# Weights made ready one product ahead, and a norm stage without GpSimd, in a one-core two-layer block

## The chip, the cores and the metric

The kernel runs on one core of one Trainium2 chip. The number that counts is the device time of one execution in microseconds. A core has five engines that run side by side and wait for one another by semaphores: TensorE (PE, matmuls, with a separate track PEld for loading its stationary operand), VectorE (DVE), ScalarE (ACT), GpSimd (POOL) and SyncE (SP), whose queue issues most DMAs.

## The reference, cut to what matters

One block on a sequence of 1024 tokens of width 1024, all in float32. First comes a gated DeltaNet with 8 heads of 128 and an MLP, then a final norm of the stream, then a second layer (a norm with modulation, a mixer that also reads projections of a 256-row context, a second MLP). What the change touches:

```
# DeltaNet
proj = h @ w_in                                   # q, k, v, z: 1024 columns each
q, k, v = silu(causal_depthwise_conv(proj[:3072]))# 4 taps
lower = strict(k_beta k^T * decay); solve (I + lower) [u, w] = [...]   # per 64-token chunk
state scan over 16 chunks; o = rms(o) * norm_w * silu(z)
x = x + o @ w_out                                 # part of w_out: dn_w_out[0:768]
# MLP of the first layer
x = x + square(relu(rms(x) @ w_up)) @ mlp_w_down
# between the layers: x1 = rms(x) * norm_final, then the modulated norm of x1 for layer 2
x1 = x * r1 * wf ;  h2 = x * a * r12 + sh
ctx projections: 14 products of the normed context (256 rows) with columns of w_in_2
```

Here r1 and r12 are reciprocal roots of column sums of squares (of x, and of x times wf), spread over the 128 partitions as rows.

## The kernel before, in words

Everything lies transposed: a tile is 128 features (partitions) by 512 or 1024 tokens. Matmuls keep float32 accuracy by splitting every operand into a rounded high part and a low rest: `gemm` (L149 to L151) issues three matmuls per 128 rows of weights, high by high, high by the low part of the data, and low by high. So a product with 1024 rows of weights over 512 tokens is 24 matmuls of 128x512, always in the order L149, L150, L151.

The weights of a product come from `wload`, three steps on three engines: a DMA of the raw weights on SP's queue (L138), a cast of them to the high part on ACT (L139, tile `whi`), and a subtraction on DVE that leaves the low part (L140, tile `wlo`). L149 and L150 need `whi` alone, L151 needs `wlo`. There are two buffers each for raw, high and low. A new product's raw weights can be fetched when the subtraction of the product two before has read its raw buffer.

The order of the instructions on each engine is settled when the program is built: a scheduler places them one by one, led by the order of the source, its own estimate of when operands are there, and when buffers come free. What an engine then runs is one fixed row; an instruction that waits holds up all behind it on that engine.

The stages that the change touches, in order of time in the span:

- **DeltaNet, 40 to 600 us.** Heads are worked in four pairs. For a pair: `keys` (two k projections, `project` L272, with the copy of a product out of PSUM at L285, the four-tap convolution as L288 and L290 on DVE, and silu on ACT, L292), `norms_k` (transposes L326, squares L329, the roots of L336), `prep_k` in `base` (the decay matrix `dec` L363 to L370, the products of keys L376, the matrix `N` L377, and the DMAs of its small blocks to memory and back as `A`, L382), `invert_base` (a chain of some 60 small DVE steps L396 and L400 on the 32x32 blocks `X`, which go to memory (Xd) and back as X, L415), `values` (v and q projections), `place_base` (L426 to L452, small matmuls that build the inverse `TT`, with gate products as filler between them), and `scan` (L509 to L529). While a pair is scanned, the next pair's keys and bases are made, and its v and q projections run on PE beside the DVE chain L396/L400.
- **The output projection, 600 to 690 us** (L673 to L684): 8 products with 768 rows of `dn_w_out`, each two halves of 18 matmuls. The results are copied out of PSUM by DVE (first half) and ACT (second half), L680. Beside it DVE works off the modulation vectors: long runs of L898 and L900 (`macc`), with L907 and L909 at the end of a run.
- **The first layer's last down group, 1345 to 1420 us** (`down_group`, L836, called with `done`): 16 products, 12 matmuls each, of 128 columns, the first token half first. After each, DVE adds it to x (L849), ACT squares x twice (L709), and the two sums of squares go on: one on POOL (tile `e`, L710), one on DVE (tile `fs`, L710).
- **The norms between the layers, 1410 to 1480 us** (`FirstNorms.half`, run once for each token half): sums to columns (L717, L718), roots on ACT (L202), rows (L726, L728), and then for each of 8 feature tiles f: e = x a r12 on DVE (L984), high part on ACT (L985), x r1 on POOL (L986), times wf on ACT (L987), a DMA of it out (L988), and the low part on DVE (L978). Between these steps run the 14 context products (`ctx_project` L1032), 24 matmuls of 128x256, whose weights are loaded when the product is written down; result copied by ACT, L1039. Five of them have buffers of their own for the weights (`wx`).

Of the kernel before, what the change touches and what calls it, by code (L numbers as in the profile page):

```python
# [11 lines left out]
AF = mybir.ActivationFunctionType  # L12
ALU = mybir.AluOpType
# [15 lines left out]
WX = (10, 8, 6, 4, 2)  # L29
# [176 lines left out]
def deltanet(k, spill, dbg=None):  # L206

    nc, tc, A = k.nc, k.tc, k.A
    with ExitStack() as ctx:
# [3 lines left out]
        load = load_normed(k, P, hhi, hlo)  # L213
# [4 lines left out]
        ps = k.pt((128, 96))  # L218
# [6 lines left out]
        w_in = A["dn_w_in"]  # L225
# [6 lines left out]
        W = k.wload(w_in[:, 4096:4112], cols=16)  # L232
        ps = k.pt((128, 8, 16))
        for i, sl in enumerate(HALVES):
# [21 lines left out]
            out=gl, in0=t1, scalar=-1.0, in1=ab[:, 0:1, :].to_broadcast([128, 8, 8]), op0=ALU.mult, op1=ALU.mult)  # L256
        ps = k.pt((128, 8, 8))
# [11 lines left out]

        pair = {}  # L270

        def project(h, part, out):  # L272

            W = k.wload(w_in[:, part * 1024 + h * 128: part * 1024 + h * 128 + 128])
            n = part * 8 + h
            prev = None
            for i, sl in enumerate(HALVES):
                ps = k.pg()
                k.gemm(ps, W, hhi, hlo, sl)
                pre = P.tile([128, 516], F32, tag="pre", name=k.nm("pre"), bufs=2)  # L280
                if prev is None:
                    nc.gpsimd.memset(pre[:, 0:4], 0.0)
                else:
                    nc.scalar.copy(pre[:, 0:4], prev[:, 512:516])
                nc.scalar.copy(pre[:, 4:516], ps)  # L285
                prev = pre
                acc = P.tile([128, 512], F32, tag="acc", name=k.nm("acc"), bufs=2)
                nc.vector.tensor_scalar(acc, pre[:, 4:516], convw[:, 3, n:n + 1], None, op0=ALU.mult)  # L288
                for t in (2, 1, 0):
                    nc.vector.scalar_tensor_tensor(out=acc, in0=pre[:, 1 + t:513 + t], scalar=convw[:, t, n:n + 1],  # L290
                                                   in1=acc, op0=ALU.mult, op1=ALU.add)
                nc.scalar.activation(out(i), acc, AF.Silu)  # L292
                yield
# [255 lines left out]
                    nc.vector.tensor_tensor(out=lo[:, sl], in0=z[:, sl], in1=hi[:, sl], op=ALU.subtract)  # L549

        def gates(h, pr):
            W = k.wload(w_in[:, 3072 + h * 128:3072 + h * 128 + 128])
            pr["z", h] = z = (k.xp if h % 2 else P).tile([128, 1024], F32, tag=("z", "xA")[h % 2], name=k.nm("z"), bufs=1)
            for i, sl in enumerate(HALVES):
                ps = k.pg()
                yield from k.gemm_steps(ps, W, hhi, hlo, sl)
                nc.scalar.activation(z[:, sl], ps, AF.Silu)
# [68 lines left out]
        gated = {}  # L626
# [4 lines left out]
        for p in range(4):  # L631
            pr = pair[p]
            hs = (2 * p, 2 * p + 1)
            solutions(p)
            if p == 3:
                for h in hs:
                    gated[h] = tuple(k.s1.tile([128, 1024], F32R, tag="s1", name=k.nm("o" + c)) for c in "hl")
                for h in range(6):
                    o = k.wp.tile([128, 1024], F32, tag="raw", name=k.nm("o2"), bufs=2)
# [30 lines left out]

        ms = mod.stream([0, 1, 2], [t[:, j] for t in raws for j in range(2)], nc.gpsimd, tmp)
        x = []
        for o in range(8):  # L673
            tag = ("xN", "xN", "xA", "xX", "xe", "xe", "xTT", "xTT")[o]
            x.append(k.xp.tile([128, 1024], F32, tag=tag, name=k.nm("x"), bufs=1 if tag in ("xA", "xX") else 2))
            W = k.wload(A["dn_w_out"][0:768, o * 128:o * 128 + 128], nk=6)
            for i, sl in enumerate(HALVES):
                ps = k.pg()
                k.gemm(ps, W, [gated[h][0] for h in range(6)], [gated[h][1] for h in range(6)], sl)
                (nc.scalar.copy if i else nc.vector.tensor_copy)(x[o][:, sl], ps)  # L680
                next(ms, None)
                next(ms, None)
# [5 lines left out]
HALVES = [slice(0, 512), slice(512, 1024)]  # L688
# [42 lines left out]
def dn_out_and_mlp(k, gated, mod, norms, cpd, x2d, ud, td):  # L731

    nc, A = k.nc, k.A
    x = k.x
    with ExitStack() as ctx:
        s1, s2 = k.s1, k.s2
# [62 lines left out]
        h0, cx = [], []  # L799
# [23 lines left out]
        down_group(k, A["mlp_w_down"][3584:4096], [h for h, _ in hidden], [l for _, l in hidden], xs, done=done,  # L823
                   cols=128)
        tiles = list(CTX_TILES)
        for _ in chain(h0[0], norms.half(1, HALVES[1])):
            if tiles:
                ctx_project(k, *cx, cpd, tiles.pop(0), (s1, "s1") if len(tiles) in WX else None)
        for n in tiles:
            ctx_project(k, *cx, cpd, n)  # L830


def down_group(k, wd, uhi, ulo, x, scale=None, done=None, cols=256, hook=None):


    nc = k.nc  # L836
    n = len(uhi)
    for hs in ([[0], [1]] if done is not None else [[0, 1]]):
        for o2 in range(1024 // cols):
            W = k.wload(wd[:, o2 * cols:o2 * cols + cols], nk=n, cols=cols)  # L840
            for j in range(cols // 128):
                o = cols // 128 * o2 + j
                Wj = (W[0][:, :, 128 * j:128 * j + 128], W[1][:, :, 128 * j:128 * j + 128])
                for i in hs:
                    sl = HALVES[i]
                    ps = k.pg()
                    k.gemm(ps, Wj, uhi, ulo, sl)
                    if scale is None:
                        nc.vector.tensor_tensor(out=x[o][i], in0=x[o][i], in1=ps, op=ALU.add)  # L849
                    else:  # L850
                        nc.vector.scalar_tensor_tensor(out=x[o][i], in0=ps, scalar=scale[:, o:o + 1],
                                                       in1=x[o][i], op0=ALU.mult, op1=ALU.add)
                    if done is not None:
                        done(o, i, sl)
                    if hook:
                        hook()
# [75 lines left out]
class FirstNorms:  # L932
# [15 lines left out]

    def add(self, o, i, sl):
        xs = self.x[o][:, sl]  # L950
        self.s1.add(i, xs)
        self.s2.add(i, xs, scale=self.wf[:, o:o + 1], eng=self.k.nc.vector)

    def half(self, i, sl):
        k, nc, P, x, wf, hhi, hlo = self.k, self.k.nc, self.P, self.x, self.wf, self.hhi, self.hlo
        if i == 0:
            g1 = k.vec["g_norm1_2"]
            self.a, self.sh = affine(k, g1, k.mod[:, 0:8], k.mod[:, 8:16], "a1")
            nc.vector.tensor_tensor(out=self.a, in0=self.a, in1=wf, op=ALU.mult)
        a, sh = self.a, self.sh  # L960
        c1 = P.tile([128, 4], F32, tag="c1", name=k.nm("c1"), bufs=1)
        c2 = P.tile([128, 4], F32, tag="c2", name=k.nm("c2"), bufs=1)
        if i == 0:
            self.r = self.s1p.tile([128, 2, 512], F32, tag="s1", name=k.nm("r"))
        r, nt = self.r, {}
        r1, r12 = r[:, 0, :], r[:, 1, :]
        yield
        self.s1.cols(i, c1)
        self.s2.cols(i, c2)
        rstd_cols(k, c1, c1, D, P)  # L970
        nc.vector.tensor_tensor(out=c2, in0=c2, in1=c1, op=ALU.mult)
        nc.vector.tensor_tensor(out=c2, in0=c2, in1=c1, op=ALU.mult)
        rstd_cols(k, c2, c2, D, P)
        nc.vector.tensor_tensor(out=c2, in0=c2, in1=c1, op=ALU.mult)
        rows(k, c2, r12)
        rows(k, c1, r1)
        def low(f):
            nc.vector.scalar_tensor_tensor(out=hlo[f][:, sl], in0=nt.pop(f), scalar=sh[:, f:f + 1],  # L978
                                           in1=hhi[f][:, sl], op0=ALU.add, op1=ALU.subtract)

        for f in range(8):
            xs = x[f][:, sl]
            t = nt[f] = k.e()
            nc.vector.scalar_tensor_tensor(out=t, in0=xs, scalar=a[:, f:f + 1], in1=r12, op0=ALU.mult, op1=ALU.mult)  # L984
            nc.scalar.activation(hhi[f][:, sl], t, AF.Identity, bias=sh[:, f:f + 1])  # L985
            nc.gpsimd.tensor_tensor(out=xs, in0=xs, in1=r1, op=ALU.mult)  # L986
            nc.scalar.activation(xs, xs, AF.Copy, scale=wf[:, f:f + 1])  # L987
            nc.sync.dma_start(self.x1d[f][:, sl], xs)  # L988
            if f:
                low(f - 1)  # L990
            yield
        low(7)
# [36 lines left out]
        yield  # L1029


def ctx_project(k, chi, clo, cpd, n, pool=None):  # L1032

    nc = k.nc
    W = k.wload(k.A["w_in_2"][:, 128 * n:128 * n + 128], pool=pool)
    ps = k.pg()
    k.gemm(ps[:, 0:256], W, chi, clo, slice(0, 256))
    t = k.e()[:, 0:256]
    nc.scalar.copy(t, ps[:, 0:256])  # L1039
    nc.scalar.dma_start(cpd[n], t)  # L1040
# [836 lines left out]
class Down:  # L1877
# [19 lines left out]
    def load(self, g, m):  # L1897

        k, nc = self.k, self.k.nc
        p0, n = self.groups[g]  # L1900
        for j in range(n):
            t = self.T[Up.OPERAND[m]][j]
            nc.sync.dma_start(t[:, 1].bitcast(F32), self.td[p0 + j][Up.OPERAND[m]])
        self.late.append((g, m))
        if len(self.late) > 3:
            self.split()
# [283 lines left out]
```

## Time and profile before

| what | value |
|---|---|
| median of 3 runs | 2970.7 us (2970.43 to 2975.29) |
| the profiled execution | 2967.41 us, span 2965.4 us |
| PE busy | 2790.5 us, 94% of the span |
| DVE, ACT, POOL busy | 70%, 48%, 22% |
| mean granted clock of PE | 0.983 |

The profile is of one execution, 3.3 us below the median. 2.0 us of it lie outside its span. A wait of PE is read in two ways in the rows below: as a row of the view of waits (engine, line, what it waited for: us in total, times, the longest), and in the timeline, where the bracket behind an instruction gives the idle time before it and what ended it. The mean granted clock of a stretch (PEclk) says how much of it PE spent at the lower of its two levels.

### The profile page before, as it was taken

To read this page: it belongs to the slowest core of one execution; us is meant where nothing else is said; L and a number is where in the kernel's file an instruction comes from. 1 tells how busy PE (TensorE), PEld (TensorE's weight loads), DVE (VectorE), ACT (ScalarE), POOL (GpSimd) and SP (SyncE) were. 2 spreads that over 40 slices of the span, in tenths; PEclk is the share of its full clock that TensorE was granted. 3 is DMA by queue.
4 is the path that set the end of the run, shared out by engine and by line. 5 is a ranking of instruction groups with operands and counts; after the bars stand their busy time and mean duration, and the time that the engine had idled before them with its cause. 6 is when DMAs were issued, how large, how long until landed. Compare 5 with 4: busy or idle time off the path is not lost. (4 is left out here: it accounts for less than half of the span.)

```text
span 2965.4 us, 43793 instructions
## 1 busy us (share of the span) xinstructions
PE 2790.5 (94%) x16344; PEld 2275.9 (77%) x16344; DVE 2088.1 (70%) x3343; ACT 1409.0 (48%) x2690; POOL 644.8 (22%) x578
## 2 busy tenths in 40 slices
PE   7999999989899999999899998999899999999998
PEld 5887878777677777787777777788777788887776
DVE  5877777785888887777856657677757755556784
ACT  6452636433555563435633334677645433334345
POOL 0000000011132333222422222121020322332322
PEclk9999999999899999999999999999999999999999
DMA  4313131234366774442621111001033433234433
GB/s 112 69 32 72 30 71 46 72 115 155 124 208 226 232 251 134 149 146 71 195 62 38 42 51 46 12 29 61 15 122 113 132 97 100 98 122 171 136 115 110
DMA packets 330084, 310.16 MB, mean 105 GB/s; under 512 B 36640, under 2 KB 254720, under 8 KB 329872
## 3 DMA queue, kind: packets, MB, share of 16 engines
q1 hardware_dynamic: 276880, 220.84, 24.4%
q10 hardware_dynamic: 46688, 65.52, 6.1%
q0 software_dynamic: 6304, 21.01, 3.1%
q8 instruction: 128, 2.10, 0.3%
q14 instruction: 84, 0.69, 0.1%
HBM read 232.83 MB, written 74.48 MB: 104 GB/s over the span
## 5 line engine op out<-in xcount | busy, mean ns | idle before, releaser
L1724 PE MATMUL pt<-T,blk 128*128 128x512 f32 x608 | 242.1, 400 | 12.1 <-DVE e L771 4.6
L1726 PE MATMUL pt<-T,blk 128*128 128x512 f32 x608 | 241.9, 398 | 5.4 <-DVE blk L1713 5.4
L1725 PE MATMUL pt<-T,blk 128*128 128x512 f32 x608 | 241.8, 398 | 0.7 <-DVE T L1801 0.6
L139 ACT CAST whi<-wraw 128x1024 fp32r<-128x1024 f32 (+3 forms) x126 | 116.1, 921 | 231.4 <-PE pg L150 191.4
L151 PE MATMUL pg<-dhi,wlo 128*128 128x512 f32 (+1 forms) x528 | 216.5, 411 | 10.0 <-DVE wlo L140 10.0
L149 PE MATMUL pg<-dhi,whi 128*128 128x512 f32 (+1 forms) x528 | 216.0, 409 | 0.0
L150 PE MATMUL pg<-dlo,whi 128*128 128x512 f32 (+1 forms) x528 | 214.1, 406 | 1.0 <-DVE dlo L188 1.0
L140 DVE TENSOR_TENSOR wlo<-wraw,whi 128x1024 fp32r<-128x1024 f32 (+3 forms) x125 | 138.9, 1111 | 69.5 <-ACT whi L139 67.8
L149 PE MATMUL pg<-xhi,whi 128*128 128x512 f32 x416 | 169.5, 408 | 1.4 <-ACT e L1039 1.4
L151 PE MATMUL pg<-xhi,wlo 128*128 128x512 f32 x416 | 166.5, 400 | 0.3 <-DVE wlo L140 0.3
L150 PE MATMUL pg<-xlo,whi 128*128 128x512 f32 x416 | 165.9, 399 | 0.0
L1965 PE MATMUL pt<-T,blk 128*128 128x512 f32 x368 | 146.6, 398 | 8.5 <-DVE x L1972 5.4
L1724 PEld LDWEIGHTS pt<-T,blk 128*128 128x128 f32 x608 | 115.4, 190 | 43.5 <-issue 4.6
L1967 PE MATMUL pt<-T,blk 128*128 128x512 f32 x368 | 145.6, 396 | 0.0
L1966 PE MATMUL pt<-T,blk 128*128 128x512 f32 x368 | 145.5, 395 | 0.0
L1914 DVE TENSOR_TENSOR T<-T 128x512 fp32r<-128x512 f32 x161 | 129.9, 831 | 20.4 <-ACT T L1913 20.3
L1713 DVE TENSOR_TENSOR blk<-xb,blk 128x512 fp32r<-128x512 f32 x121 | 102.4, 847 | 56.9 <-ACT blk L1712 55.2
L1726 PEld LDWEIGHTS pt<-T,blk 128*128 128x128 f32 x608 | 115.4, 190 | 32.8 <-DVE blk L1713 6.3
L1366 DVE TENSOR_TENSOR pl<-pt,ph 128x512 fp32r<-128x512 f32 x160 | 106.3, 683 | 47.2 <-ACT ph L1361 46.5
L1725 PEld LDWEIGHTS pt<-T,blk 128*128 128x128 f32 x608 | 115.7, 190 | 28.4 <-DVE T L1801 1.9
L1949 ACT CAST blk<-T 128x384 fp32r<-128x384 f32 (+1 forms) x133 | 71.9, 541 | 129.8 <-PE pt L1967 75.8
L1724 PE MATMUL ps<-T,blk 128*128 128x512 f32 x304 | 121.3, 402 | 8.8 <-ACT e L1729 4.7
(571 smaller groups left out, 7995.7 us busy)
## 6 DMA issues: line engine op xcount, KB each, us to landing
x<-w_mod SPq DMA_DIRECT2D x72, 256.0 KB, 4.4
wraw<-w_in SPq DMA_DIRECT2D x35, 512.0 KB, 4.6
T<-td SPq DMA_DIRECT2D x69, 256.0 KB, 3.3
wraw<-dn_w_in SPq DMA_DIRECT2D x32, 512.0 KB, 4.2
td<-e ACTq DMA_DIRECT2D x55, 256.0 KB, 2.0
xb<-w_gu SPq DMA_DIRECT2D x44, 256.0 KB, 3.1
wraw<-w_gu SPq DMA_DIRECT2D x22, 512.0 KB, 3.9
xin<-x SPq DMA_DIRECT2D x16, 512.0 KB, 6.1
```

Source lines behind the costliest of these rows:

```text
L139: nc.scalar.copy(hi, raw)
L140: (lo or nc.vector).tensor_tensor(out=lo_t, in0=raw, in1=hi, op=ALU.subtract)
L149: nc.tensor.matmul(out, hi[:, w, :], Hhi[k][:, sl], start=first and k == 0, stop=False)
L150: nc.tensor.matmul(out, hi[:, w, :], Hlo[k][:, sl], start=False, stop=False)
L151: nc.tensor.matmul(out, lo[:, w, :], Hhi[k][:, sl], start=False, stop=last and k == n - 1)
L1724: nc.tensor.matmul(ps, w[:, 0, j], T[j][:, 0], start=not c and j == 0, stop=False, skip_group_check=c)
L1725: nc.tensor.matmul(ps, w[:, 0, j], T[j][:, 1], start=False, stop=False, skip_group_check=c)
L1726: nc.tensor.matmul(ps, w[:, 1, j], T[j][:, 0], start=False, stop=j == 3, skip_group_check=c)
L1914: nc.vector.tensor_tensor(out=t[:, 1], in0=t[:, 1].bitcast(F32), in1=t[:, 0], op=ALU.subtract)
L1965: nc.tensor.matmul(ps, w[:, 0, j], T[j][:, 0], start=not c and j == 0, stop=False, skip_group_check=c)
L1966: nc.tensor.matmul(ps, w[:, 0, j], T[j][:, 1], start=False, stop=False, skip_group_check=c)
L1967: nc.tensor.matmul(ps, w[:, 1, j], T[j][:, 0], start=False, stop=j == n - 1, skip_group_check=c)
```

## The change

It edits five places. (1) In DeltaNet, `project` and `gates` take their weights from a function `weights` with a list of all products in the order in which they are used: whoever asks for one also makes the following one's `wload`. (2) The output projection calls `wload` for product o + 1 before the matmuls of product o. (3) `down_group` does the same, and so does (4) the run of context products, where a small `load` keeps one product ahead; `ctx_project` is handed its weights. (5) In the norm stage POOL's additions to the sum of squares go to DVE (14 instructions), and POOL's x r1 with ACT's product by wf become one DVE instruction, x wf r1 (16 of them): POOL loses 30 instructions and ACT 16. `down_group` is used by other stages too; there the order of instructions stays as it was on every engine.

```
+        todo = [(part, h) for p in range(4) for part, h in
+                ((1, 2 * p), (1, 2 * p + 1), (2, 2 * p), (0, 2 * p), (2, 2 * p + 1), (0, 2 * p + 1),
+                 (3, 2 * p), (3, 2 * p + 1))]
+        def weights(part, h):
+            n = todo.index((part, h))
+            for u in todo[n:n + 2]:
+                if u not in made:
+                    c = 1024 * u[0] + 128 * u[1]
+                    made[u] = k.wload(w_in[:, c:c + 128])
+            return made[part, h]
...
-            W = k.wload(w_in[:, part * 1024 + h * 128: part * 1024 + h * 128 + 128])
+            W = weights(part, h)
...
+        W = wout(0)
         for o in range(8):
-            W = k.wload(A["dn_w_out"][0:768, o * 128:o * 128 + 128], nk=6)
+            Wo, W = W, wout(o + 1) if o < 7 else None
...
+        nxt = load()
+        for _ in chain(h0[0], norms.half(1, HALVES[1]), range(16)):
+            if nxt:
+                now, nxt = nxt, load()
+                ctx_project(k, *cx, cpd, *now)
...
-            W = k.wload(wd[:, o2 * cols:o2 * cols + cols], nk=n, cols=cols)
+            W, nxt = nxt, load()
...
-        self.s1.add(i, xs)
+        self.s1.add(i, xs, eng=self.k.nc.vector)
...
-            nc.gpsimd.tensor_tensor(out=xs, in0=xs, in1=r1, op=ALU.mult)
-            nc.scalar.activation(xs, xs, AF.Copy, scale=wf[:, f:f + 1])
+            nc.vector.scalar_tensor_tensor(out=xs, in0=xs, scalar=wf[:, f:f + 1], in1=r1, op0=ALU.mult, op1=ALU.mult)
```

How this moves instructions is seen at three places. The first is DVE's row where the first pair is finished and the second pair's bases are prepared. Before, the low parts of two v and q products (`wlo`) stand behind both matrices `N`, and the chain on `X` (L396, L400) follows at once:

```order
L377 TENSOR_TENSOR N_2180<-pt_2189,dec_2178 128x512
L377 TENSOR_TENSOR N_2180<-pt_2203,dec_2178 128x512
L379 COPY dl_2209<-dec_2178 128x8
L290 SCALAR_TENSOR_TENSOR acc_2385<-pre_2382,convw,acc_2385 128x512
L140 TENSOR_TENSOR wlo_2393<-wraw_2391,whi_2392 128x1024
L309 TENSOR_TENSOR vs_2314<-pt_2431,nk_2105 128x512
L140 TENSOR_TENSOR wlo_2482<-wraw_2480,whi_2481 128x1024
L491 TENSOR_TENSOR kd_2059<-kd_2059,dl_2172 128x512
L396 TENSOR_TENSOR pm_2218<-X_1900,A_1899 64x31
```

Now the first of the two stands ahead of the outputs `z` of the pair that is being finished, thirteen rows ahead of the first `N`:

```order
L383 COPY glc_2185<-eg_1911 128x4
L556 SCALAR_TENSOR_TENSOR z_1339<-pt_2118,nw,z_1339 128x512
L383 COPY glc_2185<-eg_1911 128x4
L556 SCALAR_TENSOR_TENSOR z_1339<-pt_2125,nw,z_1339 128x512
L140 TENSOR_TENSOR wlo_2325<-wraw_2323,whi_2324 128x1024
L556 SCALAR_TENSOR_TENSOR z_1555<-pt_2133,nw,z_1555 128x512
L556 SCALAR_TENSOR_TENSOR z_1555<-pt_2140,nw,z_1555 128x512
L302 TENSOR_SCALAR acc_2357<-pre_2354,convw 128x512
```

And behind the last `N` come the second low part and two sets of convolution steps (`acc`) before the chain starts (L410 and L414 are L396 and L400 of before):

```order
L391 TENSOR_TENSOR N_2186<-pt_2209,dec_2184 128x512
L393 COPY dl_2215<-dec_2184 128x8
L304 SCALAR_TENSOR_TENSOR acc_2391<-pre_2388,convw,acc_2391 128x512
L140 TENSOR_TENSOR wlo_2399<-wraw_2397,whi_2398 128x1024
L304 SCALAR_TENSOR_TENSOR acc_2391<-pre_2388,convw,acc_2391 128x512
L323 TENSOR_TENSOR vs_2320<-pt_2437,nk_2111 128x512
L505 TENSOR_TENSOR kd_2065<-kd_2065,dl_2178 128x512
L302 TENSOR_SCALAR acc_2431<-pre_2428,convw 128x512
L323 TENSOR_TENSOR vs_2320<-pt_2477,nk_2111 128x512
L304 SCALAR_TENSOR_TENSOR acc_2431<-pre_2428,convw,acc_2431 128x512
L302 TENSOR_SCALAR acc_2471<-pre_2468,convw 128x512
```

So a weight's low part has moved from behind `N` to ahead of it, and convolution steps that stood between the steps of the chain on `X` now stand before it. The second place is DVE's row in the output projection. Before, the fourth product's low part stands behind the run of `macc`:

```order
L900 SCALAR_TENSOR_TENSOR macc_6290<-mraw_6128,sc,macc_6290 128x512 x2
L680 COPY x_6320<-pg_6327 128x512
L900 SCALAR_TENSOR_TENSOR macc_6290<-mraw_6128,sc,macc_6290 128x512 x2
L900 SCALAR_TENSOR_TENSOR macc_6290<-mraw_6129,sc,macc_6290 128x512 x4
L900 SCALAR_TENSOR_TENSOR macc_6290<-mraw_6130,sc,macc_6290 128x512 x2
L140 TENSOR_TENSOR wlo_6382<-wraw_6380,whi_6381 128x768
```

Now that product's low part is the first of the two here:

```order
L933 SCALAR_TENSOR_TENSOR macc_6296<-mraw_6128,sc,macc_6296 128x512 x2
L140 TENSOR_TENSOR wlo_6329<-wraw_6327,whi_6328 128x768
L699 COPY x_6326<-pg_6333 128x512
L933 SCALAR_TENSOR_TENSOR macc_6296<-mraw_6128,sc,macc_6296 128x512 x2
L933 SCALAR_TENSOR_TENSOR macc_6296<-mraw_6129,sc,macc_6296 128x512 x4
L933 SCALAR_TENSOR_TENSOR macc_6296<-mraw_6130,sc,macc_6296 128x512 x2
L140 TENSOR_TENSOR wlo_6388<-wraw_6386,whi_6387 128x768
```

It has moved ahead by eight steps of `macc` and a copy of x. The third place is PE's row at the start of the last pair's `place_base`. Before, the gate products (`pg`) are spread between its small matmuls:

```order
L149 MATMUL pg_5681<-dhi_273,whi_5675 128x512
L426 MATMUL ps_5512<-X_5428,N_4897 32x32
L150 MATMUL pg_5681<-dlo_281,whi_5675 128x512
L151 MATMUL pg_5681<-dhi_273,wlo_5676 128x512
L149 MATMUL pg_5681<-dhi_274,whi_5675 128x512
L150 MATMUL pg_5681<-dlo_282,whi_5675 128x512
L151 MATMUL pg_5681<-dhi_274,wlo_5676 128x512
L149 MATMUL pg_5727<-dhi_267,whi_5675 128x512
L150 MATMUL pg_5727<-dlo_275,whi_5675 128x512
L426 MATMUL ps_5512<-X_5428,N_4897 32x32 x15
```

Now all but three of the last gate product's matmuls stand before it, and the small matmuls follow one another (L440 is L426 of before, L448 and L450 are L434 and L436):

```order
L151 MATMUL pg_5727<-dhi_273,wlo_5466 128x512
L440 MATMUL ps_5518<-X_5434,N_4903 32x32
L149 MATMUL pg_5727<-dhi_274,whi_5465 128x512
L150 MATMUL pg_5727<-dlo_282,whi_5465 128x512
L151 MATMUL pg_5727<-dhi_274,wlo_5466 128x512
L440 MATMUL ps_5518<-X_5434,N_4903 32x32 x15
L440 MATMUL ps_5547<-X_5449,N_4940 32x32
L448 MATMUL ps_5577<-Y_5517,TT_5435 32x32
```

Twenty-six matmuls of 128x512 have moved from between the steps of that chain to ahead of it. In the row of the second pair, where the bases of the next are made, the like of it is fourteen more matmuls between the last L376 and the first L426.

## Rows read from the trace of the kernel before

**Rows 1.** The page's first part: busy us, share of the span, instructions of each engine.
```profile
PE 2790.5 (94%) x16344; PEld 2275.9 (77%) x16344; DVE 2088.1 (70%) x3343; ACT 1409.0 (48%) x2690; POOL 644.8 (22%) x578
```

**Rows 2.** Busy by stretch in DeltaNet (PE, PEld, DVE, ACT, POOL; then PEclk, DMA share, GB/s).
```profile
220.00:300.00 80.00, 71.71 (x515) 57.71 (x516) 56.83 (x128) 23.24 (x65) 4.30 (x9) 0.91 0.35 67
300.00:560.00 260.00, 245.73 (x1582) 205.51 (x1581) 194.46 (x458) 128.20 (x331) 8.09 (x22) 0.97 0.22 51
```

**Rows 3.** Waits of PE from 40 to 560 us: total us, times, longest.
```profile
PE pg L151 <- DVE wlo L140: 10.0, 3, 3.3
PE ps L426 <- DMA X<-Xd: 6.6, 2, 3.4
PE pt L376 <- DVE N L377: 6.1, 3, 2.6
```

**Rows 4.** Timeline of PE, 218 to 232 us: start, length, instruction.
```profile
229.11 0.63 PE L150 MATMUL pg<-dlo,whi 128*128 128x512 f32 x1
229.53 0.62 PE L151 MATMUL pg<-dhi,wlo 128*128 128x512 f32 x1
...
231.38 0.39 PE L149 MATMUL pg<-dhi,whi 128*128 128x512 f32 x1
231.61 0.40 PE L150 MATMUL pg<-dlo,whi 128*128 128x512 f32 x1
```

**Rows 5.** Timeline of DVE at the same place.
```profile
224.73 1.22 DVE L140 TENSOR_TENSOR wlo<-wraw,whi 128x1024 fp32r<-128x1024 f32 x1
...
233.56 0.18 DVE L396 TENSOR_TENSOR pm<-X,A 64x31 f32<-64x31 f32 x1 [5.27 <-DMA A<-Ad]
```

**Rows 6.** Timeline of ACT at the same place.
```profile
213.44 1.11 ACT L139 CAST whi<-wraw 128x1024 fp32r<-128x1024 f32 x1
```

**Rows 7.** Waits of PE from 600 to 700 us, in the output projection.
```profile
PE pg L151 <- DVE wlo L140: 5.1, 1, 5.1
PE pg L149 <- ACT x L680: 3.5, 3, 1.2
```

**Rows 8.** Timeline of DVE in the output projection.
```profile
652.64 5.38 DVE L900 SCALAR_TENSOR_TENSOR macc<-mraw,sc,macc 128x512 f32<-128x512 f32 x8
657.94 0.95 DVE L140 TENSOR_TENSOR wlo<-wraw,whi 128x768 fp32r<-128x768 f32 x1
```

**Rows 9.** Timeline of ACT in the output projection.
```profile
651.28 0.83 ACT L139 CAST whi<-wraw 128x768 fp32r<-128x768 f32 x1 [8.32 <-PE pg L150]
```

**Rows 10.** Timeline of PE in the first down group: products follow 3.25 us apart.
```profile
1384.73 0.47 PE L149 MATMUL pg<-u,whi 128*128 128x512 f32 x1
...
1387.98 0.47 PE L149 MATMUL pg<-u,whi 128*128 128x512 f32 x1 [0.18 <-DVE x L849]
```

**Rows 11.** Busy by stretch around the norms (columns as in rows 2).
```profile
1410.00:1437.00 27.00, 18.57 (x111) 16.23 (x110) 25.18 (x29) 17.02 (x28) 14.99 (x10) 0.90 0.49 151
1437.00:1450.00 13.00, 12.95 (x90) 12.75 (x91) 10.41 (x18) 8.68 (x14) 3.56 (x2) 0.82 0.79 242
1450.00:1481.00 31.00, 26.80 (x217) 25.84 (x215) 26.45 (x26) 19.92 (x32) 13.55 (x8) 1.00 0.74 226
```

**Rows 12.** Waits of PE from 1410 to 1485 us.
```profile
PE pg L151 <- DVE wlo L140: 7.0, 4, 2.8
PE pg L149 <- ACT e L1039: 4.2, 4, 1.4
```

**Rows 13.** DVE by line and form, 1375 to 1480 us: busy us, mean ns.
```profile
L978 DVE SCALAR_TENSOR_TENSOR xlo<-e,mod,xhi 128x512 fp32r<-128x512 f32 x16 | 19.1, 1201 | 1.0 <-ACT xhi L985 1.0
L710 DVE TENSOR_TENSOR fs<-fs,e 128x512 f32<-128x512 f32 x14 | 16.6, 1186 | 7.4 <-ACT e L709 7.4
L984 DVE SCALAR_TENSOR_TENSOR e<-x,a,r 128x512 f32<-128x512 f32 x16 | 15.3, 963 | 0.1
```

**Rows 14.** DVE on L710 (1385 to 1435 us) and L984: ns minimum/median/maximum.
```profile
L710 DVE TENSOR_TENSOR fs<-fs,e x11: 678/1333/1346, 1385.9 to 1429.1; 128x512 f32<-128x512 f32 x11
...
L984 DVE SCALAR_TENSOR_TENSOR e<-x,a,r x16: 734/740/1784, 1415.6 to 1476.4; 128x512 f32<-128x512 f32 x16
```

More of the change, by code (lines that the diff above doesn't have):

```diff
@@ L270, in deltanet @@
         pair = {}
+        todo = [(part, h) for p in range(4) for part, h in
+                ((1, 2 * p), (1, 2 * p + 1), (2, 2 * p), (0, 2 * p), (2, 2 * p + 1), (0, 2 * p + 1),
+                 (3, 2 * p), (3, 2 * p + 1))]
+        made = {}
+        def weights(part, h):
[5 more added lines that the diff above has]
+            return made[part, h]
         def project(h, part, out):
-            W = k.wload(w_in[:, part * 1024 + h * 128: part * 1024 + h * 128 + 128])
+            W = weights(part, h)
             n = part * 8 + h
@@ L551, in gates @@
         def gates(h, pr):
-            W = k.wload(w_in[:, 3072 + h * 128:3072 + h * 128 + 128])
+            W = weights(3, h)
             pr["z", h] = z = (k.xp if h % 2 else P).tile([128, 1024], F32, tag=("z", "xA")[h % 2], name=k.nm("z"), bufs=1)
@@ L672, in deltanet, with wout @@
         x = []
+        def wout(o):
+            return k.wload(A["dn_w_out"][0:768, o * 128:o * 128 + 128], nk=6)
+        W = wout(0)
         for o in range(8):
@@ L675, in deltanet @@
             x.append(k.xp.tile([128, 1024], F32, tag=tag, name=k.nm("x"), bufs=1 if tag in ("xA", "xX") else 2))
-            W = k.wload(A["dn_w_out"][0:768, o * 128:o * 128 + 128], nk=6)
+            Wo, W = W, wout(o + 1) if o < 7 else None
             for i, sl in enumerate(HALVES):
                 ps = k.pg()
-                k.gemm(ps, W, [gated[h][0] for h in range(6)], [gated[h][1] for h in range(6)], sl)
+                k.gemm(ps, Wo, [gated[h][0] for h in range(6)], [gated[h][1] for h in range(6)], sl)
                 (nc.scalar.copy if i else nc.vector.tensor_copy)(x[o][:, sl], ps)
@@ L825, in dn_out_and_mlp, with load @@
         tiles = list(CTX_TILES)
-        for _ in chain(h0[0], norms.half(1, HALVES[1])):
+        def load():
             if tiles:
-                ctx_project(k, *cx, cpd, tiles.pop(0), (s1, "s1") if len(tiles) in WX else None)
-        for n in tiles:
-            ctx_project(k, *cx, cpd, n)
+                n = tiles.pop(0)
+                return n, k.wload(k.A["w_in_2"][:, 128 * n:128 * n + 128], pool=(s1, "s1") if len(tiles) in WX else None)
+        nxt = load()
[3 more added lines that the diff above has]
+                ctx_project(k, *cx, cpd, *now)
 def down_group(k, wd, uhi, ulo, x, scale=None, done=None, cols=256, hook=None):
@@ L837, in down_group, with load @@
     n = len(uhi)
+    todo = [o2 for hs in range(2 if done is not None else 1) for o2 in range(1024 // cols)]
+    def load():
+        if todo:
+            o2 = todo.pop(0)
+            return k.wload(wd[:, o2 * cols:o2 * cols + cols], nk=n, cols=cols)
+    nxt = load()
     for hs in ([[0], [1]] if done is not None else [[0, 1]]):
         for o2 in range(1024 // cols):
-            W = k.wload(wd[:, o2 * cols:o2 * cols + cols], nk=n, cols=cols)
+            W, nxt = nxt, load()
             for j in range(cols // 128):
@@ L1029, in ctx_prep, with ctx_project @@
         yield
-def ctx_project(k, chi, clo, cpd, n, pool=None):
+def ctx_project(k, chi, clo, cpd, n, W):
     nc = k.nc
-    W = k.wload(k.A["w_in_2"][:, 128 * n:128 * n + 128], pool=pool)
     ps = k.pg()
```

## The prediction, made before the changed kernel had run

> **What bounds the kernel now.** I read the page's first part, then the busy time by stretch, then PE's waits in the stretches that the change touches, and last the timelines of the engines that PE waits for there. The first part is to show that PE is the bound: it is busy for 2790.5 of 2965.4 us, and no other engine comes near that [rows 1]. What a change like this can give back is therefore PE's idle time, 175 us in all, and the time that PE works at the lower of its two clock levels.
>
> In DeltaNet the waits name three releasers [rows 3]: the low part of the weights (10.0 us in three waits), the blocks X on their way back from memory (6.6 in two), the matrix N (6.1 in three). One of each falls into a pair's change to the next. Behind such a wait the matmuls run slower: their starts at 229.11 and 229.53 are 0.42 us apart, those at 231.38 and 231.61 are 0.23 apart [rows 4], which are the levels of 1.2 and 2.4 GHz. The mean granted clock is 0.91 over 71.7 busy us and 0.97 over 245.7 [rows 2], so that some 6.5 + 7.4 = 13.9 us were lost to it. All waits and all of that clock would be 22.7 + 13.9 = 36.6 us: no DeltaNet edit can give more.
>
> Why the low part is late is seen on two engines at one place: ACT had cast the high part at 213.44 [rows 6], and DVE came to the subtraction only at 224.73, eleven microseconds later [rows 5], because its row has both N ahead of it. It is DVE's order that is late there, and no transfer.
>
> **The change, part by part.**
>
> *DeltaNet.* At three changes of pair the low part now stands ahead of the z's. The cover is there: the weights are cast long before [rows 6]. So 10.0 us of waits go, and with each the half clock behind it, which I take as long as the wait that it follows, 3.4 us at half speed or 1.7 us lost: 5.1 for three. What is late next is X. PE comes to L426 earlier by 3.3 + 1.7 = 5.0 us, but does 14 matmuls more before it, 14 x 0.23 = 3.2 us, so it is there 1.8 us earlier. X must be earlier too. The chain on X starts when A lands, for which DVE sat idle 5.27 us [rows 5]; now two sets of convolution steps that stood inside the chain lie in that idle time. I have no row for a set, and price it by a DVE step of the same kind and size, 0.74 us [rows 14]: four steps, 3.0 us, or 5.9 for two sets, a little over what the hole holds. X is then some 5 us earlier, and of its 6.6 us about 6 go, with 2 us of clock behind them. N I leave as it is, since the low part that is put ahead of it takes 1.22 us [rows 5] and steps taken out from ahead of it give about that back.
>
> Against this stands the last pair: 26 matmuls, 26 x 0.23 = 6.0 us of work, were filler in `place_base`, and now are done before it. If no step of that chain waited on another engine, nothing would be lost; if each filler covered a wait, 6.0 would come back as idle time. I take the middle, 3.0. Sum: 10.0 + 5.1 + 6.0 + 2.0 - 3.0 = 20.1, **20 us**. Bounds: 36.6 at most; at least 10.0 - 6.0 = 4, if only the low part's waits go and all filler is lost, and with N and X later by what is gained, -2.
>
> *Output projection.* One wait of 5.1 us for the low part [rows 7]. DVE's subtraction at 657.94 stood behind eight steps of the modulation that take 5.38 us [rows 8]; ACT had the high part at 651.28 + 0.83 = 652.1 [rows 9]. Ahead of those steps the low part is ready at 652.1 + 0.95 = 653.1, before PE's wait began (PE waited 5.1 us up to about 658.9, so from 653.8). The whole wait goes. A copy of x out of PSUM now stands behind this subtraction, and PE waits for such copies already [rows 7]; I charge part of its 0.95 us, 0.6: **4.5 us**. Bounds: nothing (the wait moves to the copies), or 5.1 + 3.5 = 8.6.
>
> *First down group.* Products follow 3.25 us apart [rows 10] where 12 matmuls of 0.23 us need 2.73. DVE's step there is the addition to `fs`, which takes 1.333 us at the median and 0.678 at the least [rows 14]: the long ones are those beside POOL's addition to `e`. Now DVE makes both, 2 x 0.68 = 1.36: the same busy time, but the first can go while ACT still squares for the second. PE's pace becomes its own 2.73 where it had waited, in some five products that I count in the second token half: 5 x 0.52 = 2.6; **2 us**. Bounds: 0 and 8 x 0.52 = 4.2.
>
> *Norms and context.* From 1410 to 1481 us PE is idle 8.4 + 0.1 + 4.2 = 12.7 us and loses 0.10 x 18.6 + 0.18 x 13.0 = 4.2 to the clock [rows 11]: 16.9 is the upper bound. The waits are for low parts (7.0) and for PSUM copies by ACT (4.2) [rows 12]. But DVE is busy for 25.2 of the first 27 us and 62.0 of all 71 [rows 11], so the edit must be summed on DVE. Added from 1375 on: 14 additions of 0.68 and 16 steps of 0.74, that is 9.5 + 11.8 = 21.3 us. Given back, if POOL is what stretches DVE's steps: L978 16 x 0.74 = 11.8 instead of 19.1, L710 14 x 0.68 = 9.5 instead of 16.6, L984 11.8 instead of 15.3 [rows 13], together 17.9. DVE so carries 3.4 us more over 106 us, nearly what it had, while ACT loses 16 products and the waits of ACT for POOL and of x for both are gone. With the weights one ahead the 7.0 go; the 4.2 for ACT stay in part. I take **7 us**; DVE's 62.0 in 71 allow no more than about 9. Lower bound: the price in the third rival.
>
> That POOL is the cause rests on L710 alone showing two clean sizes (0.68 without, 1.33 with POOL's addition beside it). The Trainium skill, "SBUF — State Buffer", section "Who interferes with whom", states it as a rule: a DVE instruction with two inputs in SBUF and a GpSimd instruction that reads SBUF share a port, and the later one stands still until the first is done. The rows agree. By that rule all 17.9 us come back; without it nothing does, which is the third rival.
>
> *The other down groups* keep their order: 0.
>
> **The sum:** 20 + 4.5 + 2 + 7 = 33.5 us. From the profiled execution's 2967.4 that is 2933.9; the median stands 3.3 above that execution, so 2937.2, and I say **2937 us**.
>
> **The rivals.**
>
> *The gain is given back at N and X.* The chains that PE waits for (N, then A, then 60 steps, then X) are made by ACT, DVE and DMAs in series; if the low part ahead of N delays N by its 1.22 us and X does not come earlier, PE only waits later. For it: N and X together have 12.7 us of waits already, more than the low part. Against it: the 5.27 us hole. DeltaNet then gives 10.0 - 4 = 6 and with its clock still partly low no more; 6 + 4.5 + 2 + 5 = 17.5: **2953 us**.
>
> *The change hardly does what it says.* With two buffers of each kind a load can't go ahead further than these allow: in the output projection ACT sat idle 8.32 us before the cast, waiting for PE to free a buffer [rows 9]. Then the low parts come little earlier, and only the norm stage and the down group gain, 6 us: **2965 us**. Against it: the order of DVE's row did change.
>
> *Slower: DVE becomes the bound of the norm stage.* If the long steps there are long for another reason than POOL, nothing is given back. From 1410 to 1481 DVE then does 62.0 + 16 x 0.74 + 4 x 0.68 = 76.5 us, four of the additions falling behind 1410. It was busy 62.0 / 71 = 0.87 of that stretch; at the same share it takes 88 us, 17 more; and in the down group ten products come 3.25 + 0.68 us apart, 6.8 more. That eats the 24.5 of the two stages before. Below a share of 0.86 the kernel is slower; at 0.79 the stretch takes 97 us, 26 more: 2970.7 - 24.5 + 26 + 6.8 = **2979 us**. For it: DVE's steps wait on ACT in that stretch (7.4 us before L710 [rows 13]), and its share need not rise. Against it: the two clean sizes of L710.
>
> *More than forecast:* the waits for N go too and the filler is not missed: 20 + 6 + 3 in DeltaNet, 8 in the projection, 4 and 12 in the rest, 53: **2918 us**.
>
> **How the numbers follow.** Chances: forecast 0.50, given back 0.22, hardly any change 0.10, slower 0.07, more 0.11. Forecast's own range is 2925 to 2950. To leave out no more than 2 in 10, the range drops the second and third rival and holds the others: **2914 to 2960**. What this kernel's measurement can tell from no change is about 0.2%, 6 us: faster means below 2964.8. Forecast and "more" lie below it, so do nearly all of "given back" and half of "hardly": 0.50 + 0.11 + 0.20 + 0.05 = 0.86; the same 0.08 (the other half, 0.02 of "given back", 0.01 of the slower case), slower 0.06.
>
> **What will show it.** In the changed profile: the waits for L140 in DeltaNet and the projection are gone (10.0 and 5.1 to under 2); waits of L426 for X fall under 1; PEclk of 220 to 300 rises from 0.91 to 0.95 or more; `place_base` of the last pair has up to 3 us of new idle time; L710, L978 and L984 on DVE have means of 0.68 to 0.74; the stretch from the first roots to the mixer's first product is 7 us shorter. I am wrong if waits for N or X grow by what the low part's lose, if DVE's steps stay long with POOL silent, or if the last pair loses the whole 6 us at half clock.

## The result and the profile after

The changed kernel takes 2926.03 us at the median of 4 runs (2921.27 to 2929.7), the kernel before 2970.56 in the same comparison: a ratio of 0.985, 95% interval 0.9819 to 0.988, a gain of 44.5 us where 33.5 were forecast. The profiled execution is 2921.27 us with a span of 2919.4. PE is the bound as before [rows 1], with 16.4 us less of busy time for the same 16344 matmuls, and the mean granted clock is 0.988 instead of 0.983, so that more of them ran at the upper level:

```profile
PE 2774.1 (95%) x16344; PEld 2269.0 (78%) x16344; DVE 2087.7 (72%) x3373; ACT 1388.3 (48%) x2666; POOL 604.6 (21%) x548
```

To see where the time came from I compare the starts of the same matmul in both profiles:

| up to | earlier than before by | gain of the stage | forecast |
|---|---|---|---|
| the projections of the last pair | 36.6 us | | |
| the end of DeltaNet | 29.6 | 29.6 | 20 |
| the end of the output projection | 36.8 | 7.2 | 4.5 |
| 760 us, the MLP's first groups | 39.2 | 2.4 | 0 |
| the end of the MLP's other groups | 42.0 | 2.8 | 0 |
| the last down group | 44.4 | 2.4 | 2 |
| the mixer's first products | 46.2 | 1.8 | 7 |
| the end | 46.0 | -0.2 | 0 |

Such stage numbers come from one execution each. In a profile of a kernel with DeltaNet unchanged (`norms_only` below) DeltaNet ended 4.2 us later than in the profile of before (its granted clock from 220 to 300 us was 0.84 instead of 0.91), and that was gone again by 760 us. So 2 to 4 us in a stage prove nothing by themselves, and I don't explain the 2.4 and 2.8 us of the MLP, whose order is unchanged.

In DeltaNet, the waits of PE that answer to [rows 3], from 40 to 560 us (total us, times, longest). L340, L440, L390 and N's line L391 are L326, L426, L376 and L377 of before:

```profile
PE pt L340 <- ACT kT L306: 5.5, 4, 5.0
PE ps L448 <- ACT Y L443: 1.7, 2, 1.3
PE ps L460 <- ACT X L454: 1.2, 1, 1.2
...
PE ps L440 <- DMA X<-Xd: 0.2, 1, 0.2
```

The low part, N and X are gone from the list but for 0.2 us. The 5.0 us for kT were there before too and the change doesn't touch them. New are short waits in the last pair's `place_base` (L448, L460). The busy time by stretch (PE, PEld, DVE, ACT, POOL, then PEclk) answers to [rows 2]:

```profile
220.00:300.00 80.00, 79.78 (x625) 65.86 (x624) 65.15 (x142) 28.25 (x75) 4.47 (x10) 1.00 0.35 67
300.00:540.00 240.00, 239.16 (x1546) 201.70 (x1546) 196.97 (x470) 115.19 (x332) 7.92 (x21) 1.00 0.23 56
540.00:575.00 35.00, 30.50 (x382) 27.12 (x381) 20.75 (x36) 18.27 (x35) 0.53 (x1) 0.80 0.38 110
```

PE is full and at the upper level from 220 to 540 us. What was lost is all in the third row: the last pair's `place_base`, 4.5 us idle and a granted clock of 0.80. The same matmuls in both kernels, before and after:

```profile
575.00:602.00 27.00, 26.07 (x369) 21.25 (x368) 19.30 (x31) 17.22 (x32) 0.00 (x0) 1.00 0.40 119
538.50:572.40 33.90, 29.41 (x368) 25.91 (x367) 20.39 (x38) 17.19 (x32) 0.53 (x1) 0.80 0.35 103
```

They take 6.9 us more: 3.6 us of idle time, and 3.3 us of longer busy time at the lower clock.

Why N no longer stops PE is seen at the place of [rows 4 to 6]. DVE's timeline after:

```profile
212.79 1.22 DVE L140 TENSOR_TENSOR wlo<-wraw,whi 128x1024 fp32r<-128x1024 f32 x1
...
222.69 1.28 DVE L391 TENSOR_TENSOR N<-pt,dec 128x512 f32<-128x512 f32 x2
```

The low part is ready at 214.0 instead of 226.0, and N is made at the very time at which it was made before. PE's timeline there:

```profile
215.07 2.92 PE L390 MATMUL pt<-kT 128*128 128x128 f32 x24
217.75 0.49 PE L150 MATMUL pg<-dlo,whi 128*128 128x512 f32 x1
218.07 0.40 PE L151 MATMUL pg<-dhi,wlo 128*128 128x512 f32 x1
...
221.53 1.05 PE L390 MATMUL pt<-kT 128*128 128x128 f32 x8
```

Between the products of keys whose PSUM DVE must first empty (that was the wait for N) PE now runs sixteen matmuls of the next projection, which could not go on without the low part. So one early weight covers N's wait too; `q_ahead_only` below tests that.

In the output projection the 5.1 us are gone and the copies' 3.5 stay [rows 7]:

```profile
PE pg L149 <- ACT x L699: 3.5, 3, 1.2
PE pg L773 <- DMA xin<-x: 2.8, 4, 1.2
```

The granted clock of the stage is 1.00 (570 to 653 us) instead of 0.96 (600 to 690 us before). No run undoes the second edit alone, but the stage's gain goes with it: -0.5 us in `dn_only` below, which lacks it, 7.1 in `ahead_only`, which has it.

In the norm stage, DVE by line and form from 1331 to 1436 us (busy us, mean ns), against [rows 13]. L1011, L729 and L1017 are L978, L710 and L984 of before; L1019 is the new product x wf r1, and the first L729 row the additions that POOL made before:

```profile
L1011 DVE SCALAR_TENSOR_TENSOR xlo<-e,mod,xhi 128x512 fp32r<-128x512 f32 x16 | 12.0, 752 | 3.3 <-ACT xhi L1018 3.3
L1017 DVE SCALAR_TENSOR_TENSOR e<-x,a,r 128x512 f32<-128x512 f32 x16 | 11.9, 752 | 0.1
L1019 DVE SCALAR_TENSOR_TENSOR x<-x,vcols,r 128x512 f32<-128x512 f32 x16 | 11.9, 751 | 0.0
...
L729 DVE TENSOR_TENSOR e<-e,e 128x512 f32<-128x512 f32 x14 | 9.7, 691 | 0.9
L729 DVE TENSOR_TENSOR fs<-fs,e 128x512 f32<-128x512 f32 x14 | 9.7, 691 | 0.0
```

With GpSimd silent all steps have the short size [rows 14]. The three lines that took 19.1 + 16.6 + 15.3 = 51.0 us now take 12.0 + 9.7 + 11.9 = 33.6, and the two added ones 11.9 + 9.7 = 21.6: 55.2 together, 4.2 us more. PE's waits from 1380 to 1460 us, against [rows 12]:

```profile
PE pg L149 <- DVE x L882: 4.6, 1, 4.6
PE pg L149 <- ACT e L1070: 3.1, 3, 1.9
PE pg L151 <- DVE wx L140: 1.2, 1, 1.2
PE pg L151 <- DVE wlo L140: 1.0, 3, 0.5
```

The low parts' 7.0 us are down to 1.0 (and 1.2 for `wx`), but the first context products now wait for PSUM until DVE has added the last down products to x (L882): that addition stands behind DVE's new norm steps.

### The profile page after: what moved, and what is told of

Its sections match the earlier page's. It is cut to its first block, busy times and chain, and to the rows that moved or that the text cites. A ratio compares the mean times of both kernels' runs of the same rounds, so it can differ in the third digit from the quotient of the medians.

```text
span 2919.4 us, 43740 instructions
## 1 busy us (share of the span) xinstructions
PE 2774.1 (95%) x16344; PEld 2269.0 (78%) x16344; DVE 2087.7 (72%) x3373; ACT 1388.3 (48%) x2666; POOL 604.6 (21%) x548
```

## The experiments

**One edit at a time.** The first run takes the first edit alone, the second only this line of it, by which one weight in eight is made ahead:

```
-            for u in todo[n:n + 2]:
+            for u in todo[n:n + (2 if part == 2 and h % 2 == 0 else 1)]:
```

> The kernel before with the first edit alone (DeltaNet's weights one product ahead). From the two profiles DeltaNet ends 29 us earlier after the change. Theory: that comes from this edit alone, so the time is 2970.6 - 29 = 2941 us, up to 3 us less for changes of clock further on; the waits of PE for the low part, for X and for N in DeltaNet are gone as in the changed kernel. Rival: part of the 29 us needs the other edits (the output projection's loads, which come right behind), then 2948 us or more.

> The kernel before with the weights of one product in eight made ahead: the first q product of each pair, whose load is placed at the start of the first v product; all others are made when they are used, as before. Theory: a change of pair lost its time to this one low part, which stood behind N on DVE, and the rest followed from it; then the time is that of all products ahead, 2938 to 2942 us, with the same order of PE's instructions. Rival: every product's lead counts, one in eight gives a third of the gain or less, 2960 us.

Measured beside the kernel before (2967.61 us there): `dn_only` 2935.84, ratio 0.9896 (0.9877 to 0.9916); `q_ahead_only` 2939.12, ratio 0.9901 (0.9882 to 0.992). The first edit alone gives 32 us and one weight per pair gives 28.5; the intervals overlap. By its time `dn_only` is below the 2938 to 2941 us of its theory, but the kernel before ran 3 us faster here than the 2970.6 from which the theory counted. In the profile of `q_ahead_only` DeltaNet ends 30.1 us earlier than before, in that of `dn_only` 29.5. The low part, N and X are gone from the waits of both, while the projection's wait stays, as that edit is not in them (`q_ahead_only`, 600 to 700 us):

```profile
PE pg L151 <- DVE wlo L140: 5.1, 1, 5.1
PE pg L149 <- ACT x L693: 3.5, 3, 1.2
```

Both theories of these two runs held: DeltaNet's gain is the first q product's low part of each pair, and that the others are ahead too adds nothing that can be told.

**The norms without GpSimd, alone and left out.** `norms_only` is the kernel before with the fifth edit; `ahead_only` the changed kernel with it undone (POOL's x r1, ACT's product by wf and POOL's additions are back).

> The kernel before with the fifth edit alone (POOL's 30 instructions to DVE, ACT's 16 gone, weights loaded as before). Theory: POOL's instructions stretched DVE's, so DVE does the added work in the time that it gets back; medians of the additions to fs, of e and of the low part fall to 0.68 to 0.75 us, and the first down group gains 2.4 us as in the changed kernel; the norm stage gains nothing or little: 2965 to 2969 us. Rival: DVE carries 21 us more in a stage that it bounds, and the kernel is slower, 2975 us or more.

> The changed kernel with its fifth edit undone: all weights one ahead, the norms with GpSimd as before. Theory: the norms without GpSimd are worth 2 to 5 us, so this is 2928 to 2931 us. Rival: in the changed kernel PE newly waits 4.6 us for an addition to x that stands behind DVE's added work, so the fifth edit costs time once the weights are early: 2921 to 2924 us.

`norms_only` took 2959.89 us, ratio 0.9973 (0.9957 to 0.9988): faster by 8 us, more than the theory allowed. `ahead_only` took 2932.55, ratio 0.9879 (0.9859 to 0.9898), 6 us above the changed kernel by time and 9 by ratio, with overlapping intervals, and just outside its theory's 2928 to 2931. The stage from 1365 us to the mixer tells more: 7.4 us shorter than before in `norms_only` (where its theory gave 2.4 to the down group and little to the norms), the same length to 0.1 us in `ahead_only`, although all its weights are one ahead, and 4.2 us shorter in the changed kernel. PE's waits there, 1330 to 1450 us in `ahead_only`:

```profile
PE pg L151 <- DVE wlo L140: 7.0, 4, 2.8
PE pg L151 <- DVE wx L140: 2.7, 3, 1.1
```

and 1400 to 1480 us in `norms_only`, where the weights are not ahead:

```profile
PE pg L149 <- DVE x L849: 5.9, 2, 4.6
...
PE pg L151 <- DVE wlo L140: 1.5, 3, 0.7
```

The 7.0 us are still there with the weights ahead, and fall to 1.5 without that, when GpSimd is silent. So the low parts were late because DVE's row was slow, not because they were asked for late. The fifth edit also takes 16 products off ACT, but that is not it: DVE waits for ACT's casts of these weights for 4.3 us before and 3.7 in `norms_only` (1410 to 1485 us), while the longest subtraction for a low part falls from 2.28 to 1.23 us. Neither rival held.

**The third and fourth edit undone,** all else changed:

> The changed kernel with its third and fourth edit undone: the down groups' and the context products' weights are loaded when they are used, as before; all else changed. Theory: in that stage the low parts were late since DVE's steps were stretched by GpSimd, and not since they were asked for late, so that these two edits bring nothing: 2923 to 2927 us. Rival: they bring a part of the 7 us of waits for low parts, 2930 us or more.

2920.5 us, ratio 0.9846 (0.9825 to 0.9866), not to be told from the changed kernel's 0.985; its stage from 1320 us to the mixer is 1.6 us shorter. These two edits bring nothing that can be measured; the theory held. In this run and the next three the kernel before took 2965.37 us, 5 us less than the 2970.6 from which their theories count, so the ratios are the better measure.

**GpSimd at work for nobody.** To the changed kernel:

```
+            nc.gpsimd.tensor_tensor(out=self.scr, in0=r1, in1=r12, op=ALU.mult)
```

once per feature tile and half, into a tile that nothing reads.

> The changed kernel with 16 products of r1 and r12 on GpSimd added in the norm stage, into a tile that nothing reads; nothing waits for them but the next r. Theory: GpSimd's instruction alone stretches the DVE instruction beside it, so the steps L1017, L1019 and the low parts that run beside one take 1.2 to 1.8 us instead of 0.75, some 8 to 16 us more DVE time in the stage, and the time is 2930 to 2936 us. Rival: the long steps of before came from something else (waits for ACT's tiles, bank conflicts with the loads); then DVE's durations stay at 0.75 and the time at 2926 us.

2941.02 us, ratio 0.9918 (0.9896 to 0.9941), 15 us slower than the changed kernel by time and 20 by ratio. DVE by line and form, 1331 to 1470 us (L1012, L1018 and L1020 are L1011, L1017 and L1019 of the changed kernel):

```profile
L1020 DVE SCALAR_TENSOR_TENSOR x<-x,vcols,r 128x512 f32<-128x512 f32 x16 | 16.5, 1034 | 0.0
L1012 DVE SCALAR_TENSOR_TENSOR xlo<-e,mod,xhi 128x512 fp32r<-128x512 f32 x16 | 16.1, 1004 | 3.6 <-ACT xhi L1019 3.6
L1018 DVE SCALAR_TENSOR_TENSOR e<-x,a,r 128x512 f32<-128x512 f32 x16 | 16.0, 1003 | 0.1
```

Means rise from 0.75 to 1.0 us, 12.8 us for these three lines, with the sums of squares 16. The stage is 17 us longer (3.6 us behind the changed kernel at 1320 us, 20.3 at 1440). So the cause of the long steps in [rows 13, 14] is shown: an instruction of GpSimd beside them. The price was above the theory's 4 to 10 us. It arrived on PE in two parts: over the same matmuls (1366 to 1436 us in the changed kernel, 1369.6 to 1456.4 here) PE is idle for 24.9 us instead of 11.9, and busy for 61.9 instead of 58.2 at a granted clock of 0.82 instead of 0.95. The largest of its waits, 5.9 us in the changed kernel, is for DVE's additions to x:

```profile
PE pg L149 <- DVE x L882: 13.8, 2, 9.3
```

**The first half's norm steps begun later,** behind the down group's last products:

```
-            if i == 1 and o > 2:
+            if i == 1 and o > 5:
                 next(h0[0], None)
```

> The changed kernel with the first half's norm steps placed behind the last products of the down group instead of between them (begun at the seventh product of the second token half instead of the fourth). Theory: the two waits of PE for additions to x (1.3 and 4.6 us) come from DVE's added steps standing ahead of these additions, and go; the context's products start 5 us earlier, but the norms end at the same time or a little later, and the gain is 0 to 4 us: 2922 to 2926 us. Rival: DVE's work in the stage is the bound, and starting it later costs what it starts later, 2929 us or more.

2919.06 us, ratio 0.9842 (0.9821 to 0.9862). The two waits for additions to x (5.9 us together in the changed kernel) are gone from the list of 1330 to 1450 us, whose longest is now

```profile
PE pg L149 <- ACT e L1070: 2.6, 4, 1.9
```

and the stage from 1320 us to the mixer is 5.7 us shorter than in the changed kernel. The mechanism held; in the whole time it can't be told from the changed kernel's 0.985.

**The chain on X in the last pair.** Left out here are two of the four convolution taps of that pair's v and q:

```
-                for t in (2, 1, 0):
+                for t in (2, 1, 0) if part in (1, 3) or h < 6 else (0,):
```

> The changed kernel with two of the four convolution taps left out for the last pair's v and q (16 DVE steps of 0.74 us, 11.8 us, that stand between the steps of the chain on X). Theory: in the last pair PE came 36.6 us earlier to the small matmuls than before, X only 30.5 us, and what was between them was lost; with X earlier by up to 11.8 us DeltaNet ends 6 to 7 us earlier than in the changed kernel, 2919 us. Rival: the loss is the bare chain of small matmuls at half clock and has nothing to do with X: DeltaNet ends at the same time, 2926 us.

2919.14 us, ratio 0.9839 (0.9819 to 0.9859). X's DMAs are issued at 537.26 us instead of 543.03, gate products stand between the steps of `place_base` again, and DeltaNet ends 6.9 us earlier than in the changed kernel: 29.6 + 6.9 = 36.5, all of the lead that PE had. The stretch of `place_base`:

```profile
540.00:575.00 35.00, 34.44 (x431) 29.33 (x431) 23.52 (x49) 20.19 (x44) 0.00 (x0) 1.00 0.34 100
```

PE 34.4 of 35 us busy at full clock, instead of 30.5 at 0.80. In the changed kernel, the late X was the bound of the last pair, and the bare chain with its idle time and lower clock was what that cost. With the taps gone all of DVE's row behind them is earlier too; this run does not tell X's arrival from that.

**Trying for a better kernel.** On one chip, beside the changed kernel: the later norm start with the third and fourth edit undone; the later start with the first tap of the last pair's v and q on ACT; the same for all pairs.

```
+                if h > 5 and part in (0, 2):
+                    nc.scalar.activation(acc, pre[:, 4:516], AF.Copy, scale=convw[:, 3, n:n + 1])
+                else:
                     nc.vector.tensor_scalar(acc, pre[:, 4:516], convw[:, 3, n:n + 1], None, op0=ALU.mult)
```

> The changed kernel as it is, for comparison with the three beside it: its ratio to the kernel before again 0.985, within 0.003.

> The changed kernel with the first half's norm steps begun later, and with the third and fourth edit undone. Theory (those two edits bring nothing; the later start takes PE's waits for additions to x away, 5.7 us in the stage): 3 to 6 us below the changed kernel beside it. Rival: with the additions early, PE wants the context's low parts sooner, and now they are late: as the changed kernel, or slower.

> The changed kernel with the later start of the first half's norms, and with the first of the four taps of the last pair's v and q convolutions on ACT (8 DVE steps of 0.48 us, 3.8 us, out of the chain on X; ACT is busy less than half of that time). Theory: X comes up to 3.8 us earlier and DeltaNet ends up to 3.8 us earlier; with 3 to 6 us from the norms, 5 to 9 us below the changed kernel beside it. Rival: the tap on ACT waits in ACT's row and delays the convolution, so that X gains nothing: 3 to 6 us below.

> As the run before, but with the first tap on ACT for the v and q products of all four pairs. Theory: X is late in the last pair alone (PE waits 0.2 us for it in the others), so that the three other pairs gain nothing: within 2 us of the run before. Rival: DVE's row bounds every pair, and 2 to 3 us more are gained in each.

| run | median us | ratio to before (2964.42) | interval |
|---|---|---|---|
| `changed_again` | 2926.50 | 0.9871 | 0.985 to 0.9892 |
| `half_later_edits_undone` | 2924.30 | 0.9863 | 0.9841 to 0.9884 |
| `tap_act_half_later` | 2920.73 | 0.9848 | 0.9824 to 0.9871 |
| `tap_act_all` | 2928.42 | 0.9878 | 0.9856 to 0.99 |

`changed_again` is within 0.003 of 0.985, as expected. None of the others beats the changed kernel clearly; 5.8 us is the most, with overlapping intervals. The later start shortens its stage by 6.6 us in the second run and 7.3 in the third, but the whole time shows a third of the first, 2.2 us, less than the theory's 3 to 6. The tap on ACT did not do what it was for: in the third run X's DMAs came 1.9 us earlier and PE was 1.0 us ahead up to 563 us, yet DeltaNet ended 1.3 us later. Between lie matmuls at the lower clock; from 564 to 568 us, the changed kernel and then the third run (columns as in [rows 2]):

```profile
564.00:568.00 4.00, 4.00 (x35) 3.95 (x36) 3.99 (x6) 3.22 (x7) 0.00 (x0) 1.00 0.17 50
564.00:568.00 4.00, 4.00 (x23) 4.00 (x23) 2.15 (x4) 2.50 (x4) 0.00 (x0) 0.57 0.32 87
```

Why the clock rose later there is open. The run's 5.8 us lie in the range of its theory (5 to 9) and of its rival (3 to 6); DeltaNet's end speaks against the theory, so the time is no support for it. With all pairs DeltaNet ended 12.7 us later, with waits for X back (40 to 600 us):

```profile
PE ps L443 <- DMA X<-Xd: 4.4, 2, 3.0
```

So the theory of `tap_act_all`, that the other pairs don't care, fell, and so did its rival's gain. The convolution itself waits for the tap on ACT for only 1.5 us there; what grew are DVE's waits for other work of ACT from 40 to 600 us, above all for the cast of the weights, which is 5.1 us in the changed kernel:

```profile
DVE wlo L140 <- ACT whi L139: 14.6, 9, 4.5
```

That the taps in ACT's row made these casts late is likely and not shown. At the mixer this run is 4.2 us behind `changed_again` and at the end of the span level with it; the later norm start explains most of the first, and nothing here explains the rest.

## Why the prediction was right, and where its sum was not

- **What bounds it:** right. The gain in DeltaNet came from the two things named, PE's waits and its clock; the bound of 36.6 us was reached at the last pair's projections. That it fits to 0.1 us is chance, since its clock term comes from means of two digits and is good to 1 or 2 us.
- **The low part's waits, 10.0 and 5.1 us:** gone, as forecast. One reading was off: 213.44 is where the cast begins; it ends at 214.55, so that DVE came ten microseconds behind it, not eleven, and the argument stands. In the projection 7.2 us came instead of 4.5: I had priced the clock behind such waits in DeltaNet and left it out here.
- **X, 6 of 6.6 us:** 6.4 came.
- **N: the step that failed.** "N I leave as it is" looked at when N is made, which did not change, and not at what PE can do meanwhile. The early low part let 16 matmuls into the gap: 6.1 us and the clock behind them. These 6.1 us and the clock, 1.00 where I expected 0.95 (all 13.9 us came back, not 7.1), are the 13 us by which PE led more than forecast (36.6 against 23.1).
- **The last pair, -3.0: mis-sized.** It was -7.0, more than the 6.0 that I gave as all of the filler lost, and one of my signs of being wrong came true here. The idle time was nearly as forecast, 3.6 us; the clock behind it, another 3.3 us, I had put at nothing. The mechanism was the rival's of the gain given back at X, in this pair alone; `taps_cut` bears that out.
- **The down group, 2 us:** 2.4, from the fifth edit as forecast: 2.4 in `norms_only`, 0.1 in `ahead_only`.
- **The norm stage, 7 us: a wrong reason.** I credited the 7.0 us to weights one ahead and only a hiding place to the removal of GpSimd. The runs show the opposite: from 1365 us to the mixer, down group included, 0 from the first and 7.4 from the second. All edits together gave 4.2 there, 1.8 of it behind the down group, less than the fifth edit alone; that PE newly waits for additions to x is part of it, and `half_later` gets 5.7 back.
- **DVE's balance:** right. 17.9 us back were forecast for three lines, 17.4 came, and 21.6 were added for 21.3 forecast.
- **The rivals:** that DVE becomes the bound and the kernel slower is refuted by the short sizes with GpSimd silent; that the change hardly does what it says, by `q_ahead_only`.
- **Luck:** DeltaNet's lead was 13 us above the forecast and its loss 4 us above, the projection brought 2.7 us more, the norms 5.2 us less, and 5 us came in stages forecast at 0. That the sum is only 11 us off is in part such errors cancelling.

## What to carry to other kernels

When PE waits in turn for several things at one place, ask first which of them also locks up work that could fill the other gaps: one low part that stood a few rows too late on VectorE cost its own 3.3 us, the wait beside it, and the clock behind both. A gain ahead of a chain of other engines is kept only up to the point where that chain becomes the bound, so compare the two leads. And before loading earlier what comes late, look whether the engine that makes it is being slowed: here a GpSimd instruction running beside it was the cause.

## What I had not expected of the hardware

GpSimd work that nobody waits for is not free: 16 instructions of 1.63 us raised the mean of 48 VectorE steps beside them from 0.75 to 1.0 us and lengthened the stage by 17 us. The Trainium skill, "SBUF — State Buffer", section "Who interferes with whom", says that a VectorE instruction with two inputs in SBUF contends with a GpSimd instruction that reads SBUF. This run agrees: all three lines are such steps, and GpSimd's product reads r1 and r12. VectorE's stretch was 16 us, with the sums of squares; on TensorE it came out as 13 us more of idle time and a granted clock of 0.82 instead of 0.95.
